# Feed-forward weights split with ScalarE and an accumulating DMA instead of VectorE, for two of seven operands

## The chip, the cores and the metric

The kernel runs on one core of one Trainium2 chip. The metric is the time of one execution on the device in microseconds (us), as the median of several runs; less is better. A core has five engines that run side by side and wait for each other by semaphores: TensorE (PE: matmuls, and PEld: its weight loads), VectorE (DVE), ScalarE (ACT), GpSimd (POOL) and SyncE (SP). SP and POOL issue DMAs here, which 16 DMA engines carry out. SBUF is the on-chip memory of 128 partitions; PSUM holds the matmuls' sums.

## The reference

Two layers of an encoder over 512 tokens of width 1024, float32 throughout. Each layer has two feed-forwards, and these are what matters here (four in all, hidden width 2816):

```python
def swiglu(x, w_gate, w_up, w_down):
    return (jax.nn.silu(x @ w_gate) * (x @ w_up)) @ w_down

for i in range(DEPTH):
    y = swiglu(x, ffn_w_gate[i, 0], ffn_w_up[i, 0], ffn_w_down[i, 0])
    x = layer_norm(ALPHA * x + 0.5 * y, ln_g[i, 0], ln_b[i, 0])
    ...
    y = swiglu(x, ffn_w_gate[i, 1], ffn_w_up[i, 1], ffn_w_down[i, 1])
    x = layer_norm(ALPHA * x + 0.5 * y, ln_g[i, 3], ln_b[i, 3])
```

Between the two stand the layer's token mixing (windowed, global or neighbourhood attention) and an attention over 256 memory tokens.

## The kernel before

**Three matmuls for one.** Every operand of a large matmul is split in two float32r parts: a high part, which is the operand rounded to that type by a cast on ACT, and a low part, the operand less its high part, by a subtraction on DVE (`split`, lines 364 to 373). `mm3` (line 375) then multiplies high by high, high by low and low by high, in the order in which the third of each three reads the weights' low part.

**Groups and products.** A feed-forward's hidden columns are taken in groups (`ffn`, line 873). The first group is multiplied plainly; four groups of 2 x 256 columns go through `quarters` (line 696), once for the gate matrix and once for the up matrix. There the product of a 1024 x 512 block of weights with the tokens is made by seven products of blocks half as large in both directions, numbered in the order 1, 6, 5, 2, 7, 4, 3, instead of eight. The block's four quarters are loaded as `raw["a"]`, `raw["b"]` (lower left), `raw["c"]` and `raw["d"]` (lower right), each 512 KB as a tile of 128 x 4 x 256. Products 1, 2 and 4 use the quarters a, b and d as they are; 6, 5, 7 and 3 use sums of quarters. One of these sums is made by a DMA that adds to what lies in SBUF (`plus`, line 647, issued by POOL): `raw["a"]` plus quarter b, for product 3. Each product is 24 matmuls of 256 columns.

**Down products.** `down_steps` (line 766) does the same with the down weights of the group before, 7 products in 2 halves of 6 matmuls of 512 columns; two more accumulating DMAs of POOL prepare its operands. The steps of both kinds alternate: a hidden product, half a down product, and so on.

**Stages of a step.** A step is a triple of load, prep and product. `staged` (line 862) runs the load of step j, the prep of step j - 2 and the product of step j - 3 together, counted over hidden and down steps. `prep(m)` splits the weights of product m (`wide`, line 642) into `left[m]`, and `product(m)` reads them.

**What sets the order.** These calls only record operations. `Graph.plan` (line 182) then orders each engine's instructions with a table of estimated costs, twice; the second time the operations of DVE, ACT and POOL are keyed by how late each may end (`deadlines`, line 276). Tiles of one tag are granted in the order of the calls. The tag `slab` has 27 buffers of 4 KB per partition (line 341), and raw weights, high and low parts all live there, so the order of allocation decides how early a preparation may start. Since every recorded operation is issued at one line, the profile has line 157 for nearly all instructions; they are told apart by engine, operation and the names of their tiles.

The lines that decide about the operands:

```python
left[m] = self.wide(raw[{1: "a", 6: "a", 5: "u", 2: "b", 7: "v", 4: "d", 3: "a"}[m]])
if m == 6:
    self.plus(raw["a"], w, 1, c1)
```

Of the kernel before, what the change touches and what calls it, by code (L numbers as in the profile page):

```python
# [12 lines left out]
F32 = mybir.dt.float32  # L13
F32R = mybir.dt.float32r
BF16 = mybir.dt.bfloat16
I32 = mybir.dt.int32
AF = mybir.ActivationFunctionType
# [3 lines left out]
P = 128  # L21
# [299 lines left out]
class Kernel:  # L321
# [320 lines left out]
    def wide(self, z):  # L642
        got = [self.slab(F32R, tuple(z.shape)) for _ in range(2)]
        self.split(z, *got)
        return got

    def plus(self, z, w, q, c):
        self.nc.gpsimd.dma_start(out=z, in_=w[512 * q : 512 * q + 512, c : c + 256].rearrange("(k p) f -> p k f", p=P), accum_op=ALU.add)
        return z

    def mix(self, dst, x, y, op):
        self.nc.vector.tensor_tensor(out=dst, in0=x, in1=y, op=op)
        return dst
# [42 lines left out]
    def quarters(self, w, c1, c2, xs, h, gate, up):  # L696


        nc, mix = self.nc, self.mix
        flat = lambda z: z.rearrange("p b n -> p (b n)")  # L700
        raw, left, own = {}, {}, {}
        fill, onto = (1, 6, 5), {2: 1, 7: 6, 4: 6, 3: 5}
        def load(m):
            if m == 1:
                raw["a"] = self.quarter(w, 0, c1)
            elif m == 6:
                raw["c"] = self.quarter(w, 0, c2)
                raw["d"] = self.quarter(w, 1, c2)
            elif m == 2:
                raw["b"] = self.quarter(w, 1, c1)  # L710

        def prep(m):
            if m == 6:
                raw["v"] = mix(self.slab(F32, (P, 4, 256)), raw["a"], raw["c"], ALU.add)
                raw["u"] = mix(raw["c"], raw["c"], raw["d"], ALU.add)
                mix(raw["a"], raw["a"], raw["u"], ALU.add)
            left[m] = self.wide(raw[{1: "a", 6: "a", 5: "u", 2: "b", 7: "v", 4: "d", 3: "a"}[m]])
            if m == 6:
                self.plus(raw["a"], w, 1, c1)

        def done(f, s, z):
            if up:
                if not h:
                    h.extend(self.slab(F32, (P, 2, 2, 256)) for _ in range(2))
                mix(flat(h[f][:, s]), z, gate[f, s], ALU.mult)
            else:
                y = self.t2(F32) if s == 0 else z
                nc.scalar.activation(y, z, AF.Silu)
                gate[f, s] = y

        def product(m):
            if m in fill:
                own[m] = self.ps("a")
            ps, wt = own[onto.get(m, m)], left.pop(m)
            for b in range(2):
                for k in range(4):
                    self.mm3(
                        ps[:, b * 256 : b * 256 + 256], [z[:, k, b * P : (b + 1) * P] for z in wt],
                        [z[:, k, :] for z in xs[m]], m in fill and b == 0 and k == 0, k == 3, skip_group_check=True,
                    )  # L740
            if m == 1:
                own["c12"], own["c22"] = self.t2(F32), self.t2(F32)
                nc.scalar.copy(own["c12"], ps)
            elif m == 6:
                mix(ps, ps, own["c12"], ALU.subtract)
                nc.scalar.copy(own["c12"], ps)
            elif m == 5:
                nc.scalar.copy(own["c22"], ps)
            elif m == 7:
                mix(own["c22"], ps, own["c22"], ALU.subtract)  # L750
                done(1, 1, own["c22"])
            elif m == 3:
                mix(own["c12"], ps, own["c12"], ALU.subtract)
                done(0, 1, own["c12"])
            else:
                done(int(m == 4), 0, ps)

        bound = lambda f, m: lambda: f(m)
        return [tuple(bound(f, m) for f in (load, prep, product)) for m in (1, 6, 5, 2, 7, 4, 3)]

    def split_pair(self, z, scale=None):
# [4 lines left out]
    def down_steps(self, h, w, r1, r2, coef, u2, last, fresh=False, alone=False):  # L766
# [26 lines left out]
        def prep(m):  # L793
            if m == 6:
                raw["t1"] = mix(self.slab(F32, (P, 2, 512)), raw["12"], raw["11"], ALU.add)
                raw["t2"] = mix(self.slab(F32, (P, 2, 512)), raw["t1"], raw["22"], ALU.add)
                plus(raw["12"], "22")
                sums[1] = mix(self.t2(F32), act(2, 2), act(2, 1), ALU.subtract)
                sums[2] = mix(self.t2(F32), sums[1], act(1, 1), ALU.add)
            elif m == 3:  # L800
                sums[4] = mix(self.t2(F32), sums[2], act(1, 2), ALU.subtract)
            elif m == 7:
                sums[3] = mix(self.t2(F32), act(1, 1), act(2, 1), ALU.subtract)
            right[m] = self.wide(raw[{1: "11", 6: "t2", 2: "21", 5: "t1", 3: "22", 7: "12", 4: "t2"}[m]])
            if m == 6:
                plus(raw["t2"], "21")
            z = {1: lambda: act(1, 1), 2: lambda: act(1, 2), 4: lambda: act(2, 2)}.get(m) or (lambda: sums[{6: 2, 5: 1, 7: 3, 3: 4}[m]])
            left[m] = self.split_pair(z(), -1.0 if m == 6 else None)
# [857 lines left out]
```

## Time and profile before

| | |
|---|---|
| time, median of 3 runs | 2127.75 us (2125.88 to 2128.41) |
| profiled execution: span from its first to its last instruction | 2123.9 us |
| granted TensorE clock, mean over the span | 0.998 |
| DMA traffic | 275.93 MB, 130 GB/s |
| read from HBM | 259.12 MB |

The page and the trace give the profiled execution's span, and no time of its own beside it. The busy shares of the page are the time in which an engine carried out something, as a share of the span; an instruction that waits is not busy. PE and PEld overlap. The views used below are the page, the same figures for chosen stretches of time, the chain that ended last (followed back from the last instruction, at each step to what released it), groups of equal instructions with their mean duration and the idle time of the engine before them, and the instructions in order of time. In a row of the last kind, equal neighbours are merged: the start, the time until the last of them ends, the engine, the operation, written tile <- read tiles, the form, the count, and in brackets the engine's idle time before, with what ended it. Tile names are without their numbers there: `a`, `d` and `t` are PSUM banks, `slab` and `raw` SBUF tiles, `xh` and `xl` the tokens' high and low parts.

Where the four feed-forwards lie, by the names of the tiles: about 0 to 330 us, 735 to 1045, 1045 to 1390, and 1810 to the end.

### The profile page before, as it was taken

The numbers are of one execution on the slowest core, as the hardware profiler recorded it, in microseconds if no ns is written. First come the engines' busy times: TensorE is split into PE (matmuls) and PEld (weight loads), VectorE is DVE, ScalarE is ACT, GpSimd is POOL, SyncE is SP. The second block draws the span as 40 slices with busy tenths as digits, with TensorE's granted clock in tenths as the row PEclk, the third lists the DMA queues.
The fourth block names the chain that finished last, engine by engine and source line by source line (L and its number), as shares of the span: only waits on it lengthen the run. The fifth ranks groups of instructions, "written<-read, shape, count | busy, mean of one in ns | idle before, by whom it ended". The sixth has DMA issues, their size and how long they took to land.

```text
span 2123.9 us, 32745 instructions
## 1 busy us (share of the span) xinstructions
PE 2109.2 (99%) x12648; PEld 1871.0 (88%) x12648; DVE 1735.8 (82%) x2500; ACT 1161.2 (55%) x1903; POOL 287.4 (14%) x379
## 2 busy tenths in 40 slices
PE   9999999999999999999999999999999999999997
PEld 7999988888888899998889999888888888999996
DVE  7789988888748879998879999866577479699997
ACT  5555443698546554545545455457764465444552
POOL 0001015310102000000200000312210021000003
PEclk9999999999999999999999999999999999999999
DMA  6566562004434346564445556356454433456551
GB/s 205 141 168 144 136 191 91 21 18 116 140 125 109 90 117 181 150 158 129 148 100 143 126 139 186 78 147 165 119 165 155 139 93 96 110 149 155 143 149 60
DMA packets 208860, 275.93 MB, mean 130 GB/s; under 512 B 10688, under 2 KB 151616, under 8 KB 208704
## 3 DMA queue, kind: packets, MB, share of 16 engines
q1 hardware_dynamic: 175904, 221.14, 34.0%
q0 software_dynamic: 32512, 52.44, 14.1%
q8 instruction: 100, 1.64, 0.3%
q14 instruction: 56, 0.46, 0.1%
q10 hardware_dynamic: 288, 0.26, 0.0%
HBM read 259.12 MB, written 4.19 MB: 124 GB/s over the span
## 4 chain that ended last, share of the span: by engine, by line
PE 96%; DVE 1%; ACT 1%; DMA 1%; issue 0%; SPq 0%; DVEq 0%; ACTq 0%
PE a L157 59%; PE d L157 23%; PE t L157 15%; DVE slab L157 1%; ACT t L157 1%; DMA slab<-t 1%; DVE x L157 0%; ACT slab L157 0%; SPq L157 0%; DVE t L157 0%; DMA raw<-x_t 0%; ACT xh L157 0%; DVE mn L157 0%; DVE xl L157 0%; DVEq L1662 0%
## 5 line engine op out<-in xcount | busy, mean ns | idle before, releaser
L157 DVE TENSOR_TENSOR slab<-slab,slab 128x1024 fp32r<-128x1024 f32 (+3 forms) x638 | 727.5, 1166 | 69.5 <-ACT slab L157 39.9
L157 ACT CAST slab<-slab 128x1024 fp32r<-128x1024 f32 (+2 forms) x498 | 472.7, 983 | 341.5 <-DVE slab L157 173.2
L157 PE MATMUL a<-slab,slab 128*128 128x256 f32 (+3 forms) x2320 | 567.2, 322 | 0.7 <-DMA slab<-t 0.4
L157 PE MATMUL a<-xh,slab 128*128 128x256 f32 (+2 forms) x2480 | 559.9, 315 | 0.3 <-ACT slab L157 0.3
L157 PE MATMUL d<-slab,slab 128*128 128x512 f32 (+2 forms) x1856 | 447.0, 381 | 0.0
L157 PEld LDWEIGHTS a<-xh,slab 128*128 128x128 f32 x2480 | 416.4, 190 | 33.7 <-ACT slab L157 1.0
L157 PEld LDWEIGHTS a<-slab,slab 128*128 128x128 f32 x2320 | 409.5, 190 | 38.8 <-ACT t L157 1.3
L157 PE MATMUL a<-xl,slab 128*128 128x256 f32 (+1 forms) x1240 | 389.7, 314 | 0.0
L157 PE MATMUL a<-raw,slab 128*128 128x256 f32 x2048 | 388.9, 283 | 0.1
L157 PEld LDWEIGHTS d<-slab,slab 128*128 128x128 f32 x1856 | 329.0, 189 | 55.9 <-issue 0.2
L157 PEld LDWEIGHTS a<-raw,slab 128*128 128x128 f32 x2048 | 327.9, 192 | 5.4 <-ACT slab L157 0.5
L157 PEld LDWEIGHTS a<-xl,slab 128*128 128x128 f32 x1240 | 236.0, 190 | 18.4 <-DVE xl L157 0.4
L157 PE MATMUL t<-slab,slab 128*128 128x512 f32 (+1 forms) x840 | 209.5, 389 | 0.0
L157 DVE TENSOR_TENSOR slab<-raw,slab 128x1024 fp32r<-128x1024 f32 (+2 forms) x140 | 160.2, 1160 | 18.6 <-ACT slab L157 18.4
L157 PEld LDWEIGHTS t<-slab,slab 128*128 128x128 f32 x840 | 149.9, 189 | 26.3
L157 DVE TENSOR_TENSOR slab<-t,slab 128x512 fp32r<-128x512 f32 (+2 forms) x223 | 137.6, 638 | 16.4 <-ACT slab L157 15.9
L157 ACT CAST slab<-t 128x512 fp32r<-128x512 f32 (+2 forms) x223 | 120.9, 566 | 40.7 <-DVE t L157 13.9
L157 ACT CAST slab<-raw 128x1024 fp32r<-128x1024 f32 (+1 forms) x132 | 124.3, 971 | 27.9 <-PE a L157 8.8
L157 DVE SCALAR_TENSOR_TENSOR x<-d,x 128x512 f32<-128x512 f32 x168 | 114.7, 685 | 25.3 <-PE d L157 24.4
L157 ACT COPY t<-a 128x512 f32<-128x512 f32 (+1 forms) x116 | 63.5, 550 | 130.4 <-PE a L157 77.2
L157 POOL DMA_DIRECT2D slab<-ffn_w_down x40 | 47.7, 1193 | 310.3 <-DVE slab L157 276.3
L157 ACT ACTIVATE t<-a 128x512 f32<-128x512 f32 (+3 forms) x65 | 36.3, 559 | 89.0 <-PE a L157 89.0
(126 smaller groups left out, 2167.2 us busy)
## 6 DMA issues: line engine op xcount, KB each, us to landing
slab<-ffn_w_gate SPq DMA_DIRECT2D x80, 512.0 KB
slab<-ffn_w_up SPq DMA_DIRECT2D x80, 512.0 KB
slab<-ffn_w_down SPq DMA_DIRECT2D x80, 512.0 KB
slab<-ffn_w_down POOLq DMA_DIRECT2D x40, 512.0 KB, 5.8
raw<-mem_w_kv SPq DMA_DIRECT2D x16, 1024.0 KB
slab<-t SPq DMA_DIRECT2D x96, 128.0 KB
slab<-ffn_w_gate POOLq DMA_DIRECT2D x16, 512.0 KB, 7.8
slab<-ffn_w_up POOLq DMA_DIRECT2D x16, 512.0 KB, 6.0
```

The source lines that it names most:

```text
L157: op.call = lambda: fn(*args, **kw)
```

## The change

In each of the four groups and both matrices, the low parts for products 2 and 4 are made in another way. The high part is again a cast on ACT. Then ACT writes the negative of the high part into the low part's tile, and a DMA of POOL adds the quarter of the weights onto it, once more from HBM. DVE has no part in it. Both operands are prepared earlier: product 2's operand in the prep of product 5, product 4's in the prep of product 2, and quarter b is loaded with product 5 instead of 2.

```diff
+    def wide_late(self, z, w, q, c):
+
+        hi, lo = self.slab(F32R, (P, 4, 256)), self.slab(F32R, (P, 4, 256))
+        self.nc.scalar.copy(hi, z)
+        self.nc.scalar.activation(lo, hi.bitcast(F32), AF.Copy, scale=-1.0)
+        self.plus(lo, w.bitcast(F32R), q, c)
+        return [hi, lo]
+
     def plus(self, z, w, q, c):
         self.nc.gpsimd.dma_start(out=z, in_=w[512 * q : 512 * q + 512, c : c + 256].rearrange("(k p) f -> p k f", p=P), accum_op=ALU.add)
         return z
...
-            elif m == 2:
+            elif m == 5:
                 raw["b"] = self.quarter(w, 1, c1)
...
-            left[m] = self.wide(raw[{1: "a", 6: "a", 5: "u", 2: "b", 7: "v", 4: "d", 3: "a"}[m]])
+            if m not in left:
+                left[m] = self.wide(raw[{1: "a", 6: "a", 5: "u", 7: "v", 3: "a"}[m]])
             if m == 6:
                 self.plus(raw["a"], w, 1, c1)
+            elif m == 5:
+                left[2] = self.wide_late(raw["b"], w, 1, c1)
+            elif m == 2:
+                left[4] = self.wide_late(raw["d"], w, 1, c2)
```

What the planner makes of it is shown for the gate matrix of the third group in the first feed-forward, in the trace of before about 160 to 190 us. On ACT, before: slab_267 is the high part for product 5, slab_272 for product 2 (from quarter b in slab_266), slab_283 for product 7, slab_287 for product 4 (from quarter d in slab_251); the t2 and a tiles belong to products made before.

```order
L157 CAST slab_267_348<-slab_250_331 128x1024
L157 CAST slab_272_353<-slab_266_347 128x1024
L157 COPY t2_260_341<-a_259_340 128x512
L157 CAST slab_283_364<-slab_256_337 128x1024
L157 CAST slab_279_360<-slab_276_357 128x1024
L157 ACTIVATE slab_281_362<-t2_278_359 128x512
L157 COPY t2_260_341<-a_265_346 128x512
L157 CAST slab_287_368<-slab_251_332 128x1024
```

On ACT now, at the same place: slab_269 and slab_270 are the high part and the negative for product 2 (quarter b is in slab_256), slab_274 and slab_275 those for product 4, slab_285 is the high part for product 7.

```order
L157 CAST slab_267_348<-slab_250_331 128x1024
L157 CAST slab_269_350<-slab_256_337 128x1024
L157 ACTIVATE slab_270_351<-slab_269_350 128x1024
L157 CAST slab_274_355<-slab_251_332 128x1024
L157 ACTIVATE slab_275_356<-slab_274_355 128x1024
L157 COPY t2_261_342<-a_260_341 128x512
L157 CAST slab_281_362<-slab_278_359 128x1024
L157 ACTIVATE slab_283_364<-t2_280_361 128x512
L157 CAST slab_285_366<-slab_257_338 128x1024
```

The cast for product 2 keeps its place behind that for product 5; the cast for product 4 moves ahead of five rows, and two negative copies stand ahead of the copy out of bank a.

On POOL, the difference over the gate and up matrices of that group (- before, + now): slab_246 and slab_294 are the sums for product 3, slab_270, slab_275, slab_316 and slab_324 the new low parts, the rows with ffn_w_down the sums for the down products, x2 the addition of the input.

```order
 L157 DMA slab_246_327<-ffn_w_gate 128x4x256
+L157 DMA slab_270_351<-ffn_w_gate 128x4x256
+L157 DMA slab_275_356<-ffn_w_gate 128x4x256
 L157 DMA slab_253_334<-ffn_w_down 128x2x512
-L157 DMA slab_276_357<-ffn_w_down 128x2x512
+L157 DMA slab_278_359<-ffn_w_down 128x2x512
 L157 DMA slab_294_375<-ffn_w_up 128x4x256
+L157 DMA slab_316_397<-ffn_w_up 128x4x256
+L157 DMA slab_324_405<-ffn_w_up 128x4x256
 L157 DMA x2_6_87<-x 128x1x1024
```

POOL's queue, five DMAs here, has nine, and the two new ones of the gate stand ahead of both for the down products. Outside the four feed-forwards the order is the same on every engine.

## The prediction

> **What bounds the kernel now.** I read the page's busy table and chain first, then the stretches of the feed-forward, then the chain in order of time within one group of hidden columns.
>
> ```profile
> span 2123.9 us, 32745 instructions
> PE 2109.2 (99%) x12648; PEld 1871.0 (88%) x12648; DVE 1735.8 (82%) x2500; ACT 1161.2 (55%) x1903; POOL 287.4 (14%) x379
> PE 96%; DVE 1%; ACT 1%; DMA 1%; issue 0%; SPq 0%; DVEq 0%; ACTq 0%
> ...
> 49.00:108.60 59.60, 59.60 (x421) 56.04 (x420) 46.96 (x51) 33.91 (x46) 5.83 (x5) 1.00 0.55 140
> 168.60:228.20 59.60, 59.60 (x421) 56.04 (x420) 55.29 (x65) 30.26 (x39) 5.85 (x5) 1.00 0.64 150
> 753.50:992.00 238.50, 238.50 (x1681) 224.12 (x1681) 216.36 (x250) 123.06 (x155) 19.68 (x16) 1.00 0.61 156
> 1100.00:1330.00 230.00, 230.00 (x1618) 216.03 (x1617) 208.14 (x240) 117.40 (x148) 17.31 (x14) 1.00 0.59 151
> ```
>
> The last four lines are the first and third groups of the first feed-forward, the four groups of the second and most of the third. Behind the length stand PE, weight loads, DVE, ACT and POOL, the granted clock, and the DMA engines' busy share. PE is busy in every microsecond of these 587.7 us at full clock. A busy PE may still hide short waits, since ends of matmuls are modelled; the chain in order of time settles that:
>
> ```profile
> 168.75 5.75 PE a L157 x48
> 174.50 1.39 PE d L157 x6
> 175.89 2.87 PE a L157 x24
> 178.76 1.39 PE d L157 x6
> 180.15 2.87 PE a L157 x24
> 183.02 1.39 PE t L157 x6
> 184.41 2.87 PE a L157 x24
> 187.28 1.39 PE t L157 x6
> 188.67 2.87 PE a L157 x24
> ...
> 201.45 2.87 PE a L157 x24
> ```
>
> This is the gate matrix of the third group. A hidden product is 24 matmuls of 256 columns in 2.87 us (120 ns each), half a down product 6 of 512 columns in 1.39 us (232 ns). Every step takes 4.26 us to the hundredth, 14 steps make 59.64 us, and that is the group's length. Twice the columns cost about twice the time, so it is streaming, not waiting. **TensorE bounds the stretches that the change touches, without a gap.**
>
> **The change part by part.** Own time: the page gives the profiled execution its span, 2123.9 us; the median of the timed runs, 2127.75 us, is 3.85 us more, which I carry over as what lies around the span.
>
> *Removed from DVE, added to ACT.* Two operands, two matrices, four groups, four feed-forwards: 64 subtractions go, 64 negative copies come. One group's rows:
>
> ```profile
> L157 DVE TENSOR_TENSOR slab<-slab,slab 128x1024 fp32r<-128x1024 f32 x21 | 25.4, 1219 | 0.8 <-ACT slab L157 0.7
> L157 ACT CAST slab<-slab 128x1024 fp32r<-128x1024 f32 x22 | 22.6, 1050 | 19.4 <-DVE slab L157 12.5 <-PE a L157 4.9 <-issue 1.6
> ```
>
> DVE loses 64 x 1.22 = 78 us. ACT gains 64 copies; no row has this very form, and the cast of the same size, 1.05 us, gives 67 us; at worst it takes two casts, 134 us. A group holds 4 of them, 4.2 to 8.4 us against the 29 us that ACT idles of 59.6. Nothing on either engine is on the path: the 78 us lie wholly beside matmuls and are worth 0.
>
> *Added wait.* The low part is now finished by a DMA, issued by POOL. Where it lands decides, so I follow one gate matrix:
>
> ```profile
> 167.90 1.05 ACT L157 CAST slab<-slab 128x1024 fp32r<-128x1024 f32 x1 [2.34 <-DVE slab L157]
> ...
> 179.99 0.28 PE L157 MATMUL a<-xh,slab 128*128 128x256 f32 x1
> 180.10 0.28 PE L157 MATMUL a<-xl,slab 128*128 128x256 f32 x1
> 180.22 0.40 PE L157 MATMUL a<-xh,slab 128*128 128x256 f32 x2
> ...
> 188.51 0.28 PE L157 MATMUL a<-raw,slab 128*128 128x256 f32 x1
> ```
>
> The cast at 167.90 makes the high part of product 2's operand; the matmul at 180.22 is the first that reads its low part. The changed order puts this cast no later in ACT's queue and loads its weights a product earlier, so 167.90 is a late bound. Negative copy 168.95 to 170.0, POOL's DMA at 170.0: it may take 10.2 us. ACT then has cast and copy of product 4 at once, done at 172.1; product 4 begins at 188.51, its low part being read 0.24 us later: 16.6 us. What such DMAs take now, from POOL's start to landing (least, median, longest; gate, up and down in this order):
>
> ```profile
> DMA to landing us min/median/max: 5.8/7.8/9.0
> ...
> DMA to landing us min/median/max: 5.8/6.0/7.1
> ...
> DMA to landing us min/median/max: 5.5/5.8/8.9
> ```
>
> The nearest row, the gate's, says 7.8, at most 9.0. So slack is 2.4 us, at least 1.2, for product 2, and 7 or more for product 4. Cost: 0. Behind the new DMAs on POOL stand the accumulation onto the down weights, issued about 3 us later than now, and in the first feed-forward the addition of x; their readers come a group later or at its end. The two operands' pairs of slabs are also held one and two products longer, 2 x 4.26 and 2 x 8.52 us, less 8.52 for product 4's raw slab, which is let go two products earlier: 17 slab-microseconds in a matrix of 29.8 us, or 0.6 of the 27 slabs. Some 34 slabs are taken in a matrix, so a preparation finds its slab about half a microsecond later: 0 while the slack exceeds that.
>
> In the planned order PE makes two matmuls of a down product ahead of product 4 in ten of the sixteen gate matrices, and in four others one split of a down product is gone. The same matmuls in another order: 0.
>
> *Added transfers.* Their cover is the idle time of the DMA engines, and that has to be counted:
>
> ```profile
> q0 software_dynamic: 32512, 52.44, 14.1%
> ...
> 165.00:171.00 6.00, 6.00 (x42) 5.51 (x41) 6.00 (x8) 1.61 (x2) 1.32 (x1) 1.00 0.69 135
> 171.00:177.00 6.00, 6.00 (x47) 5.74 (x46) 5.93 (x8) 3.12 (x4) 1.40 (x2) 1.00 0.96 185
> 177.00:183.00 6.00, 6.00 (x46) 5.74 (x45) 5.79 (x8) 4.54 (x6) 0.98 (x1) 1.00 0.94 183
> 183.00:189.00 6.00, 6.00 (x42) 5.49 (x41) 5.30 (x8) 3.45 (x5) 0.00 (x0) 1.00 0.60 199
> 189.00:195.00 6.00, 6.00 (x47) 5.74 (x46) 5.93 (x6) 2.90 (x4) 0.00 (x0) 1.00 0.31 90
> ```
>
> POOL's queue moved 52.44 MB, 100 pieces of 512 KB, in 14.1% of 2123.9 us: 3.0 us of all 16 engines a piece. Four more per group are 12 us, and the third group's DMA share goes from 0.64 to 0.84. Between 165 and 189 the engines are busy 19.1 of 24 us already; two more pieces make 25.1, and the rest spills into the stretch behind, where 4.1 of 6 us are free. The up matrix's loads, issued from 179.96 on, come up to 6 us later. Their tightest reader is up's second product:
>
> ```profile
> 179.96 9.11 SPq L157 DMA_DIRECT2D slab<-ffn_w_up  x4
> ...
> 193.88 1.22 DVE L157 TENSOR_TENSOR slab<-slab,slab 128x1024 fp32r<-128x1024 f32 x1
> ```
>
> Its low part is done at 195.1, PE takes it up at about 201.5: 6.4 us of slack against 6 of delay. Cost 0, by a hair if all of the delay fell on these loads; they share the engines with POOL's queue, so I expect less.
>
> Sum: 2123.9 + 0 + 3.85 = 2127.75; I say **2128.0 us**, since every unknown here can only add.
>
> A page speaks against this sum. The Trainium skill, "DMA: Bandwidth & Descriptors", section "SWDGE vs HWDGE vs iDMA", says that a float32r source is read as float32, so that a float32r destination is always a cast within the DMA. The new DMAs are the first accumulations onto float32r slabs; no run here shows the price, and the page gives none. By rows it is the second rival below.
>
> **The rivals.**
>
> *DMA engines overfull (slower).* For it: shares of 0.96 and 0.94 exactly where the new pieces land. Against it: the free time behind, and the slack above. It decides once a piece costs more than about 3.2 us of the engines. At 4 us the two pieces bring 8 us: up to 1.6 us over the slack, in 16 groups up to 26 us; half of that, as loads and accumulations share the engines, gives 2141.
>
> *The accumulation onto float32r is slow (slower).* At twice the row's cost, 6 us, product 2's low part lands at 170.0 + 7.8 + 3.0 = 180.8, 0.6 us late, and up's loads up to 12 us late against 6.4: 6.2 us in 16 groups, 99 us, 2227; half of it, 2177. It decides from a landing 10.2 us after issue.
>
> *DVE is the true bound (faster).* It is busy 55.3 of 59.6 us in the third group, and if PE's busy time hid waits for it, up to 78 us would go: 2050. Against it stands the 4.26 us of every step; DVE at 46.96 in the first group gives the same 59.6. The Trainium skill, "Perfetto Trace Analysis", section "Identifying the Most-Contended Engine", says that matmul busy time is a poor measure and that weight-load busy time is to be read. That is 88% here and would leave 12%; the trace disagrees, since the steps' lengths leave none.
>
> *Nothing is moved.* Excluded: the order has 64 rows less on DVE and 64 more each on ACT and POOL.
>
> **How the numbers follow.** Forecast, PE's stream undisturbed, 0.74: 2124 to 2132. Overfull DMA engines, 0.17: 2132 to 2155, likeliest 2141. Slow float32r accumulation, 0.05: 2155 and more. DVE the bound or another gain, 0.04: below 2123.5. The range 2124 to 2142 takes in the forecast and the lower half of the first rival, 0.82 in all. A measurement here tells about 0.2%, 4.3 us, from no change: faster 0.04, same 0.74, slower 0.22.
>
> **What would show it.** Right: a group still lasts 59.6 us and its chain is PE's alone; DVE busy falls by some 78 us, ACT rises by some 67 us, POOL's queue moves 86 MB. Wrong: PE waits at the third matmul of products 2 or 4 (the accumulation is late) or at up's first or second product (loads are late). ACT's waits for the up weights, and the new pieces' landing beside 10.2 us, tell these apart. If a group is shorter than 59.6 us, the bound was misread.

## The result, and the profile after

| | before | after |
|---|---|---|
| time, median | 2127.59 us (2125.88 to 2128.41) | 2156.29 us (2155.5 to 2156.65, 4 runs) |
| ratio | | 1.0135, 95% interval 1.012 to 1.0149 |
| span of the profiled execution | 2123.9 us | 2154.4 us |
| granted TensorE clock | 0.998 | 0.996 |

The change makes the kernel 28.7 us slower, which is above the range. Lines of the page of after: the span, the busy table, the chain, POOL's queue, one group of matmuls (busy, mean ns, then the idle time ahead and its releaser) and the accumulations' median time from issue to landing:

```profile
span 2154.4 us, 32959 instructions
PE 2117.7 (98%) x12648; PEld 1875.6 (87%) x12648; DVE 1662.3 (77%) x2436; ACT 1222.6 (57%) x1967; POOL 369.8 (17%) x443
q0 software_dynamic: 66304, 85.99, 23.5%
PE 82%; DMA 8%; DVE 6%; issue 2%; ACT 2%; SPq 0%; DVEq 0%; ACTq 0%
L157 PE MATMUL a<-raw,slab 128*128 128x256 f32 x2048 | 394.2, 286 | 20.5 <-DVE t L157 20.5
slab<-ffn_w_gate POOLq DMA_DIRECT2D x48, 512.0 KB, 7.7
slab<-ffn_w_up POOLq DMA_DIRECT2D x48, 512.0 KB, 6.8
slab<-ffn_w_down POOLq DMA_DIRECT2D x40, 512.0 KB, 7.9
```

The engines' work moved as counted: DVE 73.5 us less, ACT 61.4 us more, POOL's queue at 85.99 MB. What is new is in the fifth line. In the page of before the same group had 0.1 us of idle time ahead of it:

```profile
L157 PE MATMUL a<-raw,slab 128*128 128x256 f32 x2048 | 388.9, 283 | 0.1
```

Now it is 20.5 us, and all of it is released by DVE. PE's busy time also grows by 8.5 us, part of it in this very group (394.2 against 388.9); the chain below shows what most of that is. 20.5 and 8.5 make 29.0 of the 30.5 us between the spans. The view of waits says how often (total, times, longest):

```profile
PE a L157 <- DVE t L157: 20.5, 11, 2.8
```

All eleven lie at one place of the program: the first matmul of product 4 of the gate matrix, in groups 2 to 4 of the first, third and fourth feed-forward and 3 to 4 of the second. None lies at the third matmul of products 2 or 4, where a late accumulation would show. The chain of after in the third group, in order of time (start, length, what):

```profile
182.02 7.26 DMA slab<-ffn_w_down
...
189.36 1.06 ACT slab L157
...
190.44 1.24 DVE slab L157
...
193.31 0.69 DVE t L157
...
194.05 4.53 PE a L157 x24
```

The last row is too long in itself: the 24 matmuls of a product took 2.87 us in the kernel before. Here is the same row behind another of the eleven waits, and then the 3.4 us from 195.20 on, with the granted clock as the last number but two:

```profile
257.24 3.14 PE a L157 x24
```

```profile
195.20:198.60 3.40, 3.40 (x18) 3.40 (x17) 3.37 (x4) 0.00 (x0) 0.00 (x0) 0.50 0.00 0
```

About 1 us behind the end of the wait the granted clock falls to half for 3.4 us. The same happens behind the waits that end at 904.74 and 2050.81; the three products take 4.53, 4.63 and 4.50 us, together 5.05 us more than 2.87 each. The other eight take 3.13 or 3.14, some 0.27 us more each, about 2.1 us together. That is 7.2 of the 8.5 us: the waits cost more than their idle time. The length of a wait does not tell which ones bring the fall: one of 1.84 us did and the longest, 2.80 us at 131.36, did not. What decides it was not tested.

The load at the head of the chain is that of the down quarter "21". Its cast and its subtraction follow as soon as it is there. But nothing of this is read by product 4. The link is DVE's queue, in order of time:

```profile
184.92 1.21 DVE L157 TENSOR_TENSOR slab<-slab,slab 128x1024 fp32r<-128x1024 f32 x1
190.44 1.22 DVE L157 TENSOR_TENSOR slab<-slab,slab 128x1024 fp32r<-128x1024 f32 x1 [4.30 <-ACT slab L157]
191.58 0.68 DVE L157 SCALAR_TENSOR_TENSOR slab<-t,slab 128x512 f32<-128x512 f32 x1
192.18 1.21 DVE L157 TENSOR_TENSOR slab<-slab,slab 128x1024 fp32r<-128x1024 f32 x1
193.31 0.68 DVE L157 TENSOR_TENSOR t<-a,t 128x512 f32<-128x512 f32 x1
```

The last row is the sum after product 7, which reads PSUM bank `a`. Product 4 adds onto that same bank next, and must wait until the sum has read it. And PE had done with product 7 by 189.70:

```profile
189.58 0.28 PE L157 MATMUL a<-raw,slab 128*128 128x256 f32 x1
189.70 1.55 PE L157 MATMUL t<-slab,slab 128*128 128x512 f32 x6
191.09 0.39 PE L157 MATMUL d<-slab,slab 128*128 128x512 f32 x1
191.72 0.49 PE L157 MATMUL d<-slab,slab 128*128 128x512 f32 x1 [0.24 <-DVE slab L157]
194.05 0.39 PE L157 MATMUL a<-raw,slab 128*128 128x256 f32 x1 [1.84 <-DVE t L157]
```

So the sum starts 3.6 us after its bank was ready, because an operand that waits for a load stands ahead of it, and PE runs out of down matmuls before it is done. The Trainium skill, "PSUM — Partial Sum Buffer", section "Engine vs sequencer instructions", says that VectorE's queue is strictly first in, first out; the rows agree: DVE idles 4.30 us while a sum behind the subtraction could soon have run.

Why is the load late? SP's rows, first of before, then of after (its queue's time from the first to the last issue):

```profile
165.92 6.11 SPq L157 DMA_DIRECT2D slab<-ffn_w_down  x2
```

```profile
170.47 11.92 SPq L157 DMA_DIRECT2D slab<-ffn_w_down  x2
```

The two are the loads of "22" and "21"; less the 0.37 us of an issue, "21" is issued at 171.66 before and at 182.02 after. By the end of PE's product 7 (187.12 and 189.70) that is 15.5 us ahead of it before, and 7.7 us after. And the engines that carry it are full (windows of after; the share of the 16 DMA engines is the last but one number, over 1 where packets' times overlap):

```profile
165.00:171.00 6.00, 6.00 (x40) 5.42 (x39) 5.77 (x8) 4.64 (x5) 1.28 (x1) 1.00 0.14 18
171.00:177.00 6.00, 6.00 (x51) 5.96 (x50) 4.58 (x8) 2.70 (x3) 3.81 (x3) 1.00 1.06 204
177.00:183.00 6.00, 6.00 (x41) 5.49 (x40) 6.00 (x8) 4.48 (x7) 1.20 (x1) 1.00 1.21 201
183.00:189.00 6.00, 6.00 (x47) 5.74 (x46) 3.13 (x5) 0.68 (x1) 0.00 (x0) 1.00 1.09 290
```

Before, the same stretches had 0.69, 0.96, 0.94 and 0.60. The changed kernel is 2.6 us behind by then; in stretches that start 2.58 us later it has 0.67, 1.07, 1.16 and 1.06. So two things changed at once: the load is issued later, which I put down to slabs that others take earlier, and it moves in a crowd. The experiments separate slabs, transfers and DVE's order. Three theories are tested: A, the slabs alone make the load late; B, the transfers alone do; C, both are needed. A fourth, D, came up later: the engines' time in transfers makes some load late, whichever it is, and DVE's order turns that into a wait of PE.

### The profile page after: what moved, and what is told of

Its sections match the earlier page's. It is cut to its first block, busy times and chain, and to the rows that moved or that the text cites. A ratio compares the mean times of both kernels' runs of the same rounds, so it can differ in the third digit from the quotient of the medians.

```text
span 2154.4 us, 32959 instructions
## 1 busy us (share of the span) xinstructions
PE 2117.7 (98%) x12648; PEld 1875.6 (87%) x12648; DVE 1662.3 (77%) x2436; ACT 1222.6 (57%) x1967; POOL 369.8 (17%) x443
## 3 DMA queue, kind: packets, MB, share of 16 engines
q1 hardware_dynamic: 175904, 221.14, 32.5%
q0 software_dynamic: 66304, 85.99, 23.5%
## 4 chain that ended last, share of the span: by engine, by line
PE 82%; DMA 8%; DVE 6%; issue 2%; ACT 2%; SPq 0%; DVEq 0%; ACTq 0%
PE a L157 49%; PE d L157 20%; PE t L157 13%; DMA slab<-ffn_w_down 6%; DVE slab L157 4%; ACT slab L157 1%; DVE t L157 1%; DMA slab<-ffn_w_up 1%; DVE x L157 1%; ACT t L157 1%; DMA slab<-t 1%; SPq L157 0%; DVE a L157 0%; DMA raw<-x_t 0%; ACT xh L157 0%
## 5 line engine op out<-in xcount | busy, mean ns | idle before, releaser
L157 DVE TENSOR_TENSOR slab<-slab,slab 128x1024 fp32r<-128x1024 f32 (+3 forms) x574 | 653.4, 1161 | 144.2 <-ACT slab L157 120.8
L157 PE MATMUL a<-raw,slab 128*128 128x256 f32 x2048 | 394.2, 286 | 20.5 <-DVE t L157 20.5
L157 ACT CAST slab<-raw 128x1024 fp32r<-128x1024 f32 (+1 forms) x132 | 124.4, 971 | 28.7 <-PE a L157 8.5
L157 POOL DMA_DIRECT2D slab<-ffn_w_gate x48 | 62.8, 1308 | 452.4 <-DVE slab L157 322.6
L157 DVE SCALAR_TENSOR_TENSOR x<-d,x 128x512 f32<-128x512 f32 x168 | 114.8, 686 | 20.5 <-PE d L157 19.7
L157 POOL DMA_DIRECT2D slab<-ffn_w_up x48 | 61.6, 1293 | 343.2 <-PE a L157 183.5
```

What stands on the lines that cost most here:

```text
L157: op.call = lambda: fn(*args, **kw)
```

## The experiments

Each kernel was timed beside the kernel before on the same chip; ratios are to that.

**The transfers taken out.** All orders as in the changed kernel; the 64 accumulations are recorded for the planner and not issued.

```diff
         self.plus(lo, w.bitcast(F32R), q, c)
+        self.nc.ops[-1].call = lambda: None
```

> The changed kernel with every engine's order as it is, but without the 64 new accumulations (the low parts of products 2 and 4 stay the negative high part, so the sums lack the weights there). Theory A (slabs): the two operands, taken one and two products earlier, keep slabs from the load of the down quarter "21", whose operand then comes late; the transfers do not matter. It expects the waits of PE at gate product 4 (20.5 us in all) to stay, and 2148 to 2158 us. Theory B (transfers): the 33.55 MB of new accumulations slow the loads, and the load of "21" with them. It expects those waits gone, and 2125 to 2133 us. Both together: in between, the load of "21" issued as late as in the changed kernel but landing in about 4 us instead of 7.3.

2127.04 us, ratio 1.0003 (0.9994 to 1.0012). Its waits and DVE's rows at the same place:

```profile
PE a L157 <- DVE t L157: 1.1, 1, 1.1
```

```profile
185.62 1.22 DVE L157 TENSOR_TENSOR slab<-slab,slab 128x1024 fp32r<-128x1024 f32 x1 [2.47 <-ACT slab L157]
186.77 0.68 DVE L157 SCALAR_TENSOR_TENSOR slab<-t,slab 128x512 f32<-128x512 f32 x1
187.55 1.22 DVE L157 TENSOR_TENSOR slab<-slab,slab 128x1024 fp32r<-128x1024 f32 x1
188.69 0.68 DVE L157 TENSOR_TENSOR t<-a,t 128x512 f32<-128x512 f32 x1
```

SP's row of the two loads there:

```profile
168.68 10.68 SPq L157 DMA_DIRECT2D slab<-ffn_w_down  x2
```

Theory A falls: "21" is issued at 178.99, 8.9 us ahead of the end of product 7 (187.91 here) instead of 15.5, so the earlier allocation does delay it by 6.5 us, and DVE does wait for it (2.47 us). But the sum starts 0.8 us after product 7's end, and PE finds its bank free. With the transfers "21" is issued another 1.2 us later, and takes 7.3 us instead of about 5.5 (to the start of its cast at 184.54).

**The allocation alone.** The two operands prepared as early as in the changed kernel, but with cast and subtraction.

```diff
-                left[2] = self.wide_late(raw["b"], w, 1, c1)
+                left[2] = self.wide(raw["b"])
             elif m == 2:
-                left[4] = self.wide_late(raw["d"], w, 1, c2)
+                left[4] = self.wide(raw["d"])
```

> The changed kernel's allocation (product 2's operand prepared with product 5, product 4's with product 2, quarter b loaded with product 5), but with cast and subtraction as before, no new transfer. Theory A (slabs) expects the late load of "21", PE's waits at gate product 4 and 2145 to 2165 us. Theory B (transfers) expects 2126 to 2133 us, as before the change.

2130.22 us, ratio 1.0016 (1.0007 to 1.0025): 3.6 us, an eighth of the loss. Theory A is contradicted again: the allocation is not enough. It is the weaker of the two tests, though, since "21" is issued at 175.45 here, 3.8 us later than in the kernel before, where the run without the transfers has it 7.3 us later.

**DVE's order.** The changed kernel with all its transfers; the planner must place the subtraction for "21" behind the sum of gate product 7. It plans anew with that, so other instructions move as well; on PE the two matmuls of a down product that stood ahead of product 4 join the other four behind it. That leaves the sum less time, not more.

```diff
                 mix(own["c22"], ps, own["c22"], ALU.subtract)
+                self.seven = self.nc.ops[-1]
...
             right[m] = self.wide(raw[{1: "11", 6: "t2", 2: "21", 5: "t1", 3: "22", 7: "12", 4: "t2"}[m]])
+            if m == 2:
+                self.nc.ops[-1].deps.add(self.seven)
```

> The changed kernel with one more dependency for the planner: DVE takes the subtraction for the down operand "21" only after the sum that reads the bank of gate product 7. If the wait at product 4 exists because DVE's queue is in order and the late operand stands ahead of the sum that frees the bank, the wait goes and the time falls by about 20 us to 2133 to 2142 us, although "21" is as late as it was. If the late operand itself holds PE up, the wait only moves to the down product that reads it, and the time stays at 2150 us or more. Theory B (transfers) says nothing else here.

2127.07 us, ratio 1.0002 (0.9993 to 1.0012): not 20 but all of the 28.7 us are back, since PE's busy time falls to 2109.6 us as well: with the waits, the falls of the clock are gone. Of the waits one is left, of 1.3 us, in an up matrix. SP's, ACT's and DVE's rows at the place:

```profile
167.99 11.82 SPq L157 DMA_DIRECT2D slab<-ffn_w_down  x2
```

```profile
186.36 1.05 ACT L157 CAST slab<-slab 128x1024 fp32r<-128x1024 f32 x1 [5.26 <-DMA slab<-ffn_w_down]
```

```profile
182.33 1.21 DVE L157 TENSOR_TENSOR slab<-slab,slab 128x1024 fp32r<-128x1024 f32 x1
184.54 0.69 DVE L157 SCALAR_TENSOR_TENSOR slab<-t,slab 128x512 f32<-128x512 f32 x1 [1.00 <-PE t L157]
187.42 0.69 DVE L157 TENSOR_TENSOR t<-a,t 128x512 f32<-128x512 f32 x1 [2.18 <-PE a L157]
188.03 6.89 DVE L157 TENSOR_TENSOR slab<-slab,slab 128x1024 fp32r<-128x1024 f32 x6
```

"21" is as late as in the changed kernel: it is issued at 179.44, 7.8 us ahead of the end of product 7 (187.22 here), against 7.7, and ACT waits 5.26 us for it. But the sum at 187.42 now waits for PE instead of the other way round, and the subtraction for "21" follows among the six behind it, early enough for its own reader. In this kernel POOL's queue moves the same 85.99 MB, in 24.0% of the span, and DVE keeps its 75 us of relief; the time is that of before. Nothing is gained, because DVE's relief was never on the path.

**One slab less.** The kernel before, with 26 slabs (and a tie-break that the planner then needs).

```diff
...
-    BUFS = {"t2": 14, "slab": 27, "raw": 2, "a": 3, "d": 2, "t": 3}
+    BUFS = {"t2": 14, "slab": 26, "raw": 2, "a": 3, "d": 2, "t": 3}
```

> The kernel before with 26 slabs instead of 27, no other change. The changed kernel has two operands (four slabs) ahead of the load of "21" in the allocation that stood partly behind it. Theory A (slabs) expects a later load of "21" and first waits of PE in the feed-forwards, 2135 to 2160 us. Theory B (transfers) expects no more than 4 us over the kernel before, since nothing more is moved.

2137.84 us, ratio 1.0054 (1.0037 to 1.0071). Within theory A's bounds, but not for its reason: PE has no wait for DVE's sum here; the longest is a single one of 3.3 us for an ACT cast, with 6.8 us of half clock around it, and the others are scattered, most of them outside the feed-forwards. It says that slabs are scarce in this kernel, not that they cause the loss.

**The allocation undone, the transfers kept.** All 64 low parts by copy and accumulation, but each prepared in its own product's step, and b loaded with product 2.

```diff
...
-            elif m == 5:
-                left[2] = self.wide_late(raw["b"], w, 1, c1)
-            elif m == 2:
-                left[4] = self.wide_late(raw["d"], w, 1, c2)
...
+            if m == 2:
+                left[2] = self.wide_late(raw["b"], w, 1, c1)
+            elif m == 4:
+                left[4] = self.wide_late(raw["d"], w, 1, c2)
```

> The changed way of making the low parts (copy and accumulation, all 64), but with the allocation of the kernel before: quarter b loaded with product 2, each operand prepared in its own product's step. Theory C (both needed: slabs make the load of "21" some 6.5 us later, transfers another 3, and only the sum passes the slack) expects "21" in time and no wait for DVE at gate product 4. What is left is whether the accumulations themselves land in time: product 2's low part has about 10 us by the row of the kernel before, so 2126 to 2134 us if they do, more with waits at the third matmul of products 2 or 4 if they do not. Theory B' (transfers alone suffice) expects the waits at the first matmul of gate product 4 to stay, and 2145 us or more.

2161.06 us, ratio 1.0169 (1.0152 to 1.0186): theory C falls as well, and the transfers alone suffice (B' in the text above). The profiled execution is the fastest of the four, 2154.48 us, so the waits explain that one and not the median. In it PE waits 11.4 us at the same matmul, and DVE's rows show another culprit in the same place of its queue (the chain names it: a load of the up matrix, 9.42 us from issue to landing):

```profile
182.22 9.42 DMA slab<-ffn_w_up
```

```profile
192.80 1.23 DVE L157 TENSOR_TENSOR slab<-slab,slab 128x1024 fp32r<-128x1024 f32 x1 [4.23 <-ACT slab L157]
193.94 0.68 DVE L157 TENSOR_TENSOR t<-a,t 128x512 f32<-128x512 f32 x1
```

"21" is in time now, and the first up quarter is not. A further 8.2 us are one wait in the second feed-forward, where DVE stands 8.43 us for a load of down weights, which SP issues behind 16 loads of a bias (from 816.30 on, the down weights at 835.29). The granted clock falls to half at four of these waits. The early preparation only decides which load is caught.

**One operand alone.** Product 2 alone, or product 4 alone, made in the new way; the other as before.

```diff
...
             elif m == 5:
                 left[2] = self.wide_late(raw["b"], w, 1, c1)
-            elif m == 2:
-                left[4] = self.wide_late(raw["d"], w, 1, c2)
```

> The changed kernel for product 2 alone (copy, accumulation, earlier preparation and load of b); product 4 as before. Half the new transfers; product 4's slabs are taken behind the load of "21" again. Theory C expects "21" at most 4 us later than before and no waits at gate product 4: 2126 to 2131 us. If transfers carry it alone, half of the loss: about 2142 us.

> The changed kernel for product 4 alone (prepared with product 2); product 2 as before. Half the new transfers; product 4's two slabs are taken ahead of the load of "21". Theory C expects the load of "21" issued late but landing faster than in the changed kernel: part of the waits, 2128 to 2142 us, and more than for product 2 alone. If transfers carry it alone, half of the loss, about 2142 us, for either product.

2129.8 us (1.0018, 1.0009 to 1.0028) and 2132.21 us (1.0029, 1.0018 to 1.004). Half the transfers cost 4.2 and 6.6 us, not 14: the loss is not linear in them. Waits at gate product 4: 0.3 and 2.3 us.

**One slab more.** The changed kernel with 28 slabs, 12 t2 tiles instead of 14 to make room, and the same tie-break.

```diff
...
-    BUFS = {"t2": 14, "slab": 27, "raw": 2, "a": 3, "d": 2, "t": 3}
+    BUFS = {"t2": 12, "slab": 28, "raw": 2, "a": 3, "d": 2, "t": 3}
```

> The changed kernel with 28 slabs instead of 27, and 12 instead of 14 t2 tiles to make room. Theory C expects the load of "21" issued earlier by one release of a slab (2 to 4 us), which is more than the 2.1 us by which PE waits: most of the waits gone, 2127 to 2140 us, unless the two t2 tiles are missed. Theory B (transfers alone) expects 2150 us or more.

2144.63 us, ratio 1.009 (1.0075 to 1.0105): between the two expectations. The waits for the sum are 11.1 us in 11 places; "21" is issued at 177.09 instead of 182.02, and the first up quarter, 11.4 us on its way, takes its place ahead of the sum. What the two missing t2 tiles cost was not separated.

**The dose.** Two kernels with all orders as in the changed one: each new DMA cut to its first 128 rows, a quarter of the bytes; and each new DMA a plain copy of 512 KB that overwrites the low part.

```diff
         self.plus(lo, w.bitcast(F32R), q, c)
+        dma = self.tc.nc.gpsimd.dma_start
+        self.nc.ops[-1].call = lambda: dma(out=lo[:, 0, :], in_=w.bitcast(F32R)[512 * q : 512 * q + P, c : c + 256], accum_op=ALU.add)
```

> The changed kernel with every engine's order as it is, each of the 64 new accumulations cut to its first 128 rows (a quarter of the bytes; the sums lack the weights of the other rows). Theory D (what the loads wait for is the bytes: the new accumulations take 3.23 us of the 16 DMA engines each, a load that stands before DVE's sum of product 7 lands late, and this sum frees the bank of product 4): a quarter of the bytes leaves the load of "21" within the slack, 2126 to 2134 us, waits at gate product 4 of under 5 us in all instead of 20.5. If it is the DMAs' number, their issue on POOL or their place ahead of the down weights' accumulations, the waits stay: 2145 us or more.

> The changed kernel with every engine's order as it is; the 64 new DMAs of POOL move the same 512 KB, but overwrite the low part instead of adding to it (so the low part is the weights themselves). By the busy shares of before, a plain load takes 1.66 us of the 16 engines (33.0% of 2124 us over 422 pieces), an accumulation 2.99. Theory D: what counts is the engines' time, so half of it comes back, and since the slack is passed by about 2 us only, most of the waits go: 2127 to 2140 us. If bytes from HBM count, the same as the changed kernel: 2150 us or more.

2129.99 us (1.0013, 1.0004 to 1.0023) and 2136.11 us (1.0041, 1.0026 to 1.0055). POOL's queue in the two pages:

```profile
q0 software_dynamic: 41728, 60.83, 17.0%
```

```profile
q0 software_dynamic: 66304, 85.99, 20.9%
```

Share times span, less the 299.5 us of before (14.1% of 2123.9), over 64 gives the time of all 16 engines that one new DMA takes:

| new DMAs | engines' time of each | wait of PE for the sum | time over before |
|---|---|---|---|
| none | 0 | 1.1 us | 0.5 us |
| a quarter, accumulating | 0.97 us | 2.1 us | 2.6 us |
| whole, plain | 2.29 us | 6.1 us | 8.7 us |
| whole, accumulating | 3.23 us | 20.5 us | 28.7 us |

The DMAs' number, their issue on POOL and their place ahead of the down weights' accumulations are the same in the last three rows, so these are not the cause by themselves; nor are the bytes of POOL's queue, which are the same in the last two. What orders the four rows is the engines' time, and the cost grows steeply from some 2 us a piece on, as one would expect where a delay has first to use up a slack; four points do not prove that form. The plain copy was dearer than my 1.66 us, so its expectation held only by its bounds. (The 1.66 itself was worked out from 33.0%; the page of before has 34.0%, which gives 1.71.)

**Both at once: the transfers without early preparation, and DVE's order.** The allocation of before as above, and every subtraction recorded behind a sum of product 7 stays behind it on DVE.

```diff
             nc.vector.tensor_tensor(out=lo, in0=src, in1=hi.bitcast(F32), op=ALU.subtract)
+            if hasattr(self, "seven"):
+                nc.ops[-1].deps.add(self.seven)
...
```

> The kernel with all 64 new low parts but the allocation of before (own_step: 2161 us, where DVE's sum of product 7 stands behind the split of an up quarter that landed 9.4 us after its issue), with one more dependency for the planner: no subtraction recorded behind the sum of a product 7 is taken ahead of it on DVE. Theory D expects the waits of PE for that sum at gate product 4 (11.4 us) to go, whichever load is late, and about 2145 to 2152 us, since one other wait of 8.4 us there, of ACT for a slab, is untouched. If the place of the sum in DVE's queue only mattered for the down quarter "21", nothing changes.

2145.49 us, ratio 1.0088 (1.0073 to 1.0103). The wait for the sum is gone, as theory D has it, and 15.6 us come back (by the medians; the planner moves other instructions here as well). The largest wait that is left:

```profile
PE a L157 <- DMA slab<-ffn_w_up: 10.2, 6, 3.2
```

Now late loads reach PE directly, put down to the up weights. Without early preparation the transfers are too late for more than DVE's order; with it, the order alone was enough.

## Why the prediction was wrong

*PE bounds these stretches, and DVE's 78 us are worth 0*: right. The kernel without the new transfers and the kernel with the sum in front both have DVE at 1660 to 1662 us, some 74 us less than before, and the time of before.

*The low parts come in time*: right. Gate accumulations land after 7.7 us in the median (7.8 foretold), and PE has no wait at the third matmul of products 2 or 4. The rival of a slow accumulation onto float32r falls with it, although the measured time lies where that rival had put its own: 2155 and more. The Trainium skill's rule that a float32r destination always means a cast ("DMA: Bandwidth & Descriptors", section "SWDGE vs HWDGE vs iDMA") shows at most as the 8% between 3.23 and 2.99 us of the engines; no run here separates that from crowding.

*Added transfers, 3.0 us of the engines each*: nearly right in size (3.23 measured), and the spill into crowded stretches was foretold.

*"Their tightest reader is up's second product ... 6.4 us of slack against 6 of delay. Cost 0"*: **this is the step that failed.** I asked when PE reads what a late load becomes, and that was in time: no wait of PE in the changed kernel lies at an up product. I had looked at up's loads alone, and the one that was caught in the changed kernel is the down quarter "21". The reader that counted comes earlier: the instruction that happens to stand behind the load's subtraction in DVE's queue. It is the sum after product 7, it frees the bank of product 4, and in the changed kernel it had no slack beyond the matmuls that PE has to do between the two products, one and a third half down products, 189.70 to 192.21. DVE's rows of before, which I had not weighed, showed how near this was (product 7 ended at 187.12 there):

```profile
185.88 1.22 DVE L157 TENSOR_TENSOR slab<-slab,slab 128x1024 fp32r<-128x1024 f32 x1
187.32 0.69 DVE L157 TENSOR_TENSOR t<-a,t 128x512 f32<-128x512 f32 x1 [0.23 <-PE a L157]
```

The first is the subtraction of an up quarter, and it was over 0.2 us before the sum could start. I had named what a wait holds up on PE's and POOL's queues, and not on DVE's. Nor had I a term for what a wait of PE brings behind it: about 7 us of slower matmuls beside the 20.5 us of idle time, most of it at half clock.

*"So a preparation finds its slab about half a microsecond later"*: wrong by far. An average over 27 slabs hides that they are granted in order of allocation: four taken ahead of "21" went with an issue 6.5 us later. It cost 0 alone (2127.04 us); with the transfers it chose which load was caught.

*"The same matmuls in another order: 0"*: not contradicted; PE has this order without the new transfers too, at the time of before.

*The rivals.* The first, DMA engines overfull, is what happened in its cause. That its threshold, 3.2 us a piece, lies so near the 3.23 measured is chance: it was worked out for up's second product, which never waited. 2141 us was too little, since it priced a delay of the load's own reader. It had 0.17 and deserved more: the forecast rested on one slack of 6.4 us against 6, and every other reader of the delay was left unasked.

## What to carry to other kernels

A transfer's slack is not only the time until its data are read: on an engine that works in order it is the time until anything behind the first consumer is needed, and the nearest such thing can be a bank's release for another product. When DMA engines pass from 60% to full in a stretch, list every load in it, the instruction that waits for it, and the next instructions in that queue. An engine's relief that is not on the path buys nothing, but the traffic that pays for it can cost; if it must be had, put the instructions that free the bound engine's buffers ahead of those that wait for loads. Look at the granted clock behind each wait of PE, too: the wait may not be all of its price.

## What the runs showed of the hardware

Per 512 KB, a plain load of SP took on average 1.71 us of the 16 engines in the kernel before (34.0% of 2123.9 us over 221.14 MB), a new plain copy issued by POOL 2.29 us and a new accumulation of POOL 3.23 us. Beside them the load of "21" lengthened from 5.5 us (without the transfers) to 7.3 us from issue to landing, and that of the first up quarter from about 4.1 us in the kernel before (issued at 179.96, its cast at 184.04) to 9.4 us in the kernel with the allocation undone and 11.4 us with 28 slabs, although SP's loads stand in a queue of their own. The Trainium skill, "DMA: Bandwidth & Descriptors", section "Issuing engines are not separate DMA queues", says that DMAs of all issuing engines run on the same 16 engines and interleave; these numbers agree.

Three of the eleven waits of PE in the changed kernel, 1.84 to 1.90 us long, were followed by 3.4 us in which the granted clock was 0.50. The kernel before and the two runs at its time, without the transfers and with the sum in front, had no such fall until the last 11 us of the program. In the traces of all thirteen kernels there are eleven such falls between the first 7 and the last 11 us, and each lies beside a wait of PE of 1.84 us or more.
